# Places for the attention's transposes, scores, probabilities and values, and a later norm product in RWKV

## The chip, the cores and the metric

One core of one Trainium2 chip runs the whole kernel in one launch. The metric is the device time of an execution in microseconds. A profiled execution also has a span, from its first instruction to its last, and a trace of every engine: PE (TensorE matmuls) with its weight loads (PEld), DVE (VectorE), ACT (ScalarE), POOL (GpSimd) and SP (SyncE, which here only issues DMAs).

## The reference

A decoder block over 512 tokens of width 2048, in float32, of depth 1. RWKV-7 time mixing and sliding-window attention run side by side on one projection, their outputs are gated and merged, and a gated ConvFFN follows.

```python
h = rms_norm(x, norm1_g)
z = h @ w_in                               # 2048 columns in; r, k, v, loras, q, k, v, gates out
o_rw = rwkv7_mix(token_shift(z[...]), ...) # 16 heads of 64; a state of 64x64 per head, step by step
o_att = swa_attention(q, k, v, ...)        # 16 query heads on 4 key heads, window 128, sinks
x = x + (sigmoid(zr) * (o_rw @ w_branch[:1024]) + sigmoid(za) * (o_att @ w_branch[1024:])) @ w_out
x = x + conv_ffn(rms_norm(x, norm2_g), w_up, conv_w, conv_b, w_down)

# in rwkv7_mix: kk is normalised per head before the recurrence
kk = kk / max(sqrt(sum(kk * kk)), 1e-12)
# in swa_attention: q and k are normalised per head (rms_norm), then
scores = q @ k.T / 8 + alibi;  p = softmax([scores, sink]);  o = p @ v
```

## The kernel before

Every weight matrix is read from DRAM as float32 and split into a high part (`whi`, ACT) and a rest (`wlo`, DVE). Each product is then three matmuls: high by high, high by rest, rest by high. For the first projection `project` does this per output tile of 128 columns: four weight groups (`load_w`, one DMA `raw` of 256 KB on SP, one ACT step, one DVE step, four buffers each) with 12 matmuls of 128x512 each. These matmuls, in the order in which they are written, are the list `stream`. There are 48 for an output tile. They fill PE while everything else of the branch stage (attention and RWKV) waits on other engines.

The branch work is placed between them. Tile's planner sets the order on each engine from the program and its own costs; `behind(ins, before)` adds that `ins` does not stand ahead of `before` in the order, with no semaphore, and `pin` keeps the written order among the pinned instructions. The list `held` collects pairs of an instruction and a place in `stream`; at the end each is put behind that matmul. So a number in `at`, `LEVEL` or `CHUNK` says behind how many stream matmuls a step may first stand, counted from the pair's `base`; `lag` moves a pair's places later. Engines take their queues in order: what stands first and waits holds what is behind it.

Attention, stream matmuls 0 to 720: for each of ten key and query tiles `qk_norm` squares the tile, `head_stats` sums the squares per head on PE, `rsqrt_small` takes the root on DVE in some twelve tiny steps, and `head_rows` transposes the 8 roots on PE, copies them (`rsT`), writes them to DRAM (`rsd`) and reads them back spread over the partitions (`rsb`, two DMAs on SP behind the first). Then for each of 4 groups and 4 blocks: scores (`scp`), a softmax on DVE and ACT (`sc`, `pr`), transposes of the probabilities (`mi`) and values by probabilities (`mi` from `phi` and `plo`). Three PSUM buffers `mi` go round between roots, probabilities and values.

RWKV works on eight pairs of heads. `early(p)` makes a pair's operands, `late(p)` does the recurrence in 8 chunks of 64 tokens. `early(p + 1)` is written behind `late(p)`, and both run beside each other. In `late`, a chunk n is a chain over three engines: `psG` (PE), `GY` (ACT), `psU` (PE), `UV` (half on ACT, half on DVE), `psS` (PE), and the state's update `SV` (DVE), on which the next chunk's `psG` depends. In `early`, `kk` is multiplied by the roots `rsb` on DVE (the line `kk, kk, rb`), and `kz`, `BKK` and `BAR` are made from it. `bon` and the tile `lw` are other DVE steps there; `BAR` and `BKK` are the operands of the next pair's grams (`bulk`).

Behind the last pair, pass B multiplies the branches' outputs by `w_branch` (with `project` again), and the output product `o`, then the ConvFFN, follow. For `o`, `steps_of` loads factors (`hraw`) and splits them (`hhi` on ACT, `hlo` on DVE). The first two are loaded and split while pass B still runs.

Of the kernel before, what the change touches and what calls it, by code (L numbers as in the profile page):

```python
# [14 lines left out]
ALU = mybir.AluOpType  # L15
# [4 lines left out]
P = 128  # L20
# [115 lines left out]
def block_kernel(ctx: ExitStack, tc: tile.TileContext, d: Dims, a: dict, out: bass.AP):  # L136
# [76 lines left out]
        return ins  # L213

    def split(hi, lo, src, pin=free):
        pin(act.activation(hi, src, AF.Copy))
        pin(dve.tensor_tensor(lo, src, hi.bitcast(F32) if hi.dtype == F32R else hi, op=ALU.subtract))


    def quarter(w, src, c):  # L220
# [31 lines left out]
    def behind(ins, before):  # L252
        tc.add_manual_dep(ins.ins, before.ins.name,
                          mybir.DependencyInfo(mybir.DependencyClass.NoSync, mybir.DependencyReason.DATA))

    def load_w(src):
        nk, ncol = src.shape[1:]
        n = nk * ncol
        raw = wp["raw"].tile([P, 512], F32, name="raw", tag="raw")[:, :n].rearrange("p (k c) -> p k c", c=ncol)
        wp["last"] = sync.dma_start(raw, src)  # L260
        hi = wp["hl"].tile([P, 512], F32R, name="whi", tag="whi")[:, :n].rearrange("p (k c) -> p k c", c=ncol)
        lo = wp["hl"].tile([P, 512], BF16, name="wlo", tag="wlo")[:, :n].rearrange("p (k c) -> p k c", c=ncol)
        act.activation(hi, raw, AF.Copy)  # L263
        dve.tensor_tensor(lo, raw, hi.bitcast(F32), op=ALU.subtract)  # L264
# [31 lines left out]
    if True:  # L296
# [96 lines left out]
        def head_stats(ps, sq):  # L393
            dst = ps[:, 0 : 2 * NT].rearrange("p (h t) -> p t h", h=2)
            for t in range(NT):
                pe.matmul(dst[:, t], sq[:, t * P : (t + 1) * P], K["sel2"], start=True, stop=True)

        def head_rows(pl, ps, rs, tag="lg", bufs=1):
            pe.transpose(ps[0 : 2 * NT, 0:P], rs, ident)
# [3 lines left out]
            sync.dma_start(rd, sm)  # L403
            rb = pl.tile([P, S], F32, name="rsb", tag=tag, bufs=bufs)
            src = rd.rearrange("(h t) c -> h (t c)", h=2)
            for h in range(2):
                sync.dma_start(rb[h * HD : (h + 1) * HD], src[h : h + 1].to_broadcast([HD, S]))
            return rb


        with ExitStack() as pt:
# [4 lines left out]
            def small():  # L416
                return mps.tile([P, S], F32, name="mi", tag="mi")

            unscaled = []

            def finish():

                if unscaled:
                    dst, z, rb, then = unscaled.pop()
                    pin(dve.tensor_tensor(dst, z, rb, op=ALU.mult))
                    then()

            def qk_norm(acc, gain, dst, then=lambda: None, raw=False):
                z = ap_.tile([P, S], F32, name="zq", tag="zq", bufs=3)
                if raw:  # L430
                    dve.tensor_tensor(z, acc, rowb, op=ALU.mult)
                else:
                    dve.tensor_scalar(z, acc, gain, None, op0=ALU.mult)
                sq = ap_.tile([P, S], F32, name="sqq", tag="sqq", bufs=2)
                act.activation(sq, z if raw else acc, AF.Square)
                if raw:
                    dve.tensor_scalar(z, z, gain, None, op0=ALU.mult)
                ps = small()
                head_stats(ps, sq)
                rs = rsqrt_small(ap_, ps[:, 0 : 2 * NT], 1.0 / HD, RMS_EPS)  # L440
                rb = head_rows(ap_, small(), rs, bufs=2)
                finish()
                unscaled.append((dst, z, rb, then))

# [55 lines left out]
            for g in range(NHK):  # L500
# [7 lines left out]
                for n in range(NT):  # L508
# [4 lines left out]
                    for j in range(GQ // 2):  # L513
                        for e in range(2):
                            hs = slice(e * HD, (e + 1) * HD)
                            pe.matmul(scp[e][:, j, k0:], qn[j][hs, ts],
                                      kd[g][hs, n * P - BLK + k0 : (n + 1) * P], start=True, stop=True)
# [23 lines left out]
                    for kb in kbs:  # L541
                        ps = small().rearrange("p (h c) -> p h c", c=P)
                        for h in range(GQ):
                            pe.transpose(ps[:, h % 2 * (GQ // 2) + h // 2], pr_[:, h, kb * BLK : (kb + 1) * BLK], ident)
                        split(phl[0][:, kb], phl[1][:, kb], ps)
                    ps = small()
                    for kb in kbs:
                        for i in range(2):
                            pe.matmul(ps, vhl[:, n - 1 + kb, g].rearrange("p e c -> p (e c)"),  # L549
                                      phl[i][:, kb].rearrange("p h c -> p (h c)"),  # L550
                                      start=kb == kbs[0] and i == 0, stop=kb == kbs[-1] and i == 1)
# [8 lines left out]
        with ExitStack() as pr:  # L560
# [21 lines left out]
            def bulk():  # L582
                return blk.tile([P, S], F32, name="bulk", tag="bulk")
# [41 lines left out]
            def r3(ap, c=C):  # L625
                return ap.rearrange("p (n c) -> p n c", c=c)

            def early(p):
# [12 lines left out]
                sq = wtile("lg")  # L641
                act.activation(sq, kk, AF.Square)
# [40 lines left out]
                pin(dve.tensor_tensor(kk, kk, rb, op=ALU.mult))  # L683
                dve.tensor_tensor(kb, kk, ta, op=ALU.mult)
# [4 lines left out]
                dve.tensor_tensor(bon, vz, ps, op=ALU.mult)  # L689
                return ag, Ei, kk, kb, k2, rz, vz, bon  # L690

            def late(p, st, norm, finish):
                ag, Ei, kk, kb, k2, rz, vz, bon = st
# [151 lines left out]
                for n in range(NCH):  # L845
# [21 lines left out]
                            entries.append(ins)  # L867
                    if n < NCH - 1:
                        for h, (lo, hi) in enumerate(HV):
                            dve.scalar_tensor_tensor(SV[lo:hi, n + 1, h], SV[lo:hi, n, h], ee[lo:hi, n : n + 1],  # L870
                                                     s2[lo:hi, n % HN, h], op0=ALU.mult, op1=ALU.add)
# [41 lines left out]
                dve.tensor_tensor(yc, yc, ps, op=ALU.mult)  # L913
                pool.dma_start(o_rw_d[p], yc)

            entries, grams = [], []
# [28 lines left out]
        with tc.tile_pool(name="ain", bufs=1, side="right", reuse_waits="tile") as ainp:  # L945
# [137 lines left out]
    def steps_of(w, i, acc, c, pl, got=None, flat=None):  # L1083
# [538 lines left out]
```

## Time and profile before

| what | value |
|---|---|
| median of 3 runs | 2703.35 us (2701.12 to 2705.6) |
| profiled execution, time | 2707.28 us |
| its span | 2705.4 us |
| granted TensorE clock, mean | 0.997 |
| PE busy | 2663.3 us, 98% |
| DVE, ACT, POOL busy | 2053.8, 1329.4, 458.0 us |
| attention beside the stream | about 50 to 245 us of the span |
| RWKV pairs | about 280 to 1060 us |
| pass B, output product | from about 1100 us |
| ConvFFN | from about 1450 us |

How to read it: busy PE time is matmul time, whose ends are modelled, so PE at 98% is not PE at its peak, but a hole in it is a hole. The stages have different limits; a wait counts only where PE has nothing else to do. A wait for several semaphores is put down to the one that came last.

### The profile page before, as it was taken

Reading aid. Unit: us, or ns where it says so; the run is one execution under the profiler, and the core shown is the slowest. Engines: PE = TensorE matmul, PEld = TensorE weight load, DVE = VectorE, ACT = ScalarE, POOL = GpSimd, SP = SyncE. Lnnn points to the kernel's source line nnn. Section 1 sums busy time; section 2 is a strip of 40 time slices with the busy share of each in tenths; the row PEclk is TensorE's granted clock in tenths of the full one; section 3 lists DMA queues with packets and bytes.
Section 4 is the critical chain, followed back from the end, with each engine's and each line's share of the span. In section 5 each row is a group of like instructions: output and inputs, shape, how many; then the busy total and the mean of one; then the engine's idle time right before and its main releaser. Section 6 shows DMA issues by size and latency. Waiting matters only on the chain.

```text
span 2705.4 us, 46047 instructions
## 1 busy us (share of the span) xinstructions
PE 2663.3 (98%) x17426; PEld 1870.3 (69%) x17426; DVE 2053.8 (76%) x3387; ACT 1329.4 (49%) x2229; POOL 458.0 (17%) x455
## 2 busy tenths in 40 slices
PE   8999999999999999999999999999999999999999
PEld 5555566666666666555558999999999998555555
DVE  8787758767777874545678888888888888688887
ACT  6455435445544543322456555555555555444443
POOL 0001111011111001111000111111111110166665
PEclk9999999999999999999999999999999999999999
DMA  5566888788888777878785988988898888877885
GB/s 174 157 160 186 226 202 211 192 227 218 212 211 225 193 181 180 288 240 291 255 283 164 253 243 249 255 239 237 245 253 239 237 248 258 316 248 247 265 263 190
DMA packets 227759, 619.63 MB, mean 229 GB/s; under 512 B 24896, under 2 KB 45008, under 8 KB 227024
## 3 DMA queue, kind: packets, MB, share of 16 engines
q1 hardware_dynamic: 158976, 441.03, 49.6%
q0 software_dynamic: 37216, 136.33, 26.2%
q10 hardware_dynamic: 31344, 39.31, 4.2%
q8 instruction: 137, 2.24, 0.3%
q14 instruction: 86, 0.70, 0.1%
HBM read 566.96 MB, written 191.18 MB: 280 GB/s over the span
## 4 chain that ended last, share of the span: by engine, by line
PE 90%; DVE 5%; DMA 3%; issue 1%; ACT 1%; SPq 0%; DVEq 0%; ACTq 0%; POOL 0%; POOLq 0%
PE acc L284 29%; PE X L1244 18%; PE X L1107 11%; PE Y L1107 9%; PE Y L1244 9%; PE Z L1244 4%; PE psS L864 1%; PE psG L848 1%; DMA rsb<-rsd 1%; PE bulk L770 1%; PE bulk L719 1%; DVE wlo L264 1%; PE mi L549 1%; DMA raw<-in_w_z_dram 1%; PE bulk L786 1%
## 5 line engine op out<-in xcount | busy, mean ns | idle before, releaser
L1094 DVE TENSOR_TENSOR wlo<-raw,whi 128x1024 bf16<-128x1024 f32 x210 | 308.4, 1473 | 93.2 <-ACT whi L1093 92.5
L284 PE MATMUL acc<-xhi,whi 128*128 128x512 f32 x1152 | 348.8, 427 | 9.2 <-ACT whi L263 8.9
L263 ACT ACTIVATE whi<-raw 128x512 fp32r<-128x512 f32 x352 | 218.7, 627 | 278.0 <-PE acc L284 144.8
L1093 ACT ACTIVATE whi<-raw 128x1024 fp32r<-128x1024 f32 x210 | 214.9, 1053 | 274.5 <-POOL w L1098 158.5
L264 DVE TENSOR_TENSOR wlo<-raw,whi 128x512 bf16<-128x512 f32 x352 | 239.8, 688 | 139.1 <-ACT whi L263 118.0
L284 PE MATMUL acc<-xlo,whi 128*128 128x512 bf16 x1152 | 317.3, 382 | 0.0
L284 PE MATMUL acc<-xlo,wlo 128*128 128x512 bf16 x1072 | 292.3, 380 | 0.4 <-DVE wlo L264 0.4
L1244 PEld LDWEIGHTS <-wlo 128*128 128x128 bf16 x2464 | 237.6, 96 | 39.6 <-DVE wlo L1226 0.7
L1098 POOL COPY w<-whi 128x1024 bf16<-128x1024 bf16 x132 | 224.7, 1727 | 177.1 <-ACT whi L1093 177.1
L284 PEld LDWEIGHTS acc<-xhi,whi 128*128 128x128 f32 x1152 | 213.6, 191 | 58.5 <-ACT whi L263 9.4
L1244 PEld LDWEIGHTS <-whi 128*128 128x128 bf16 x2464 | 228.0, 98 | 33.1 <-issue 0.2
L284 PEld LDWEIGHTS <-wlo 128*128 128x128 bf16 x1408 | 137.6, 99 | 151.9 <-issue 9.0
L284 PEld LDWEIGHTS <-whi 128*128 128x128 bf16 x1408 | 126.5, 101 | 149.6 <-issue 48.1
L1226 DVE TENSOR_TENSOR wlo<-raw,whi 128x1024 bf16<-128x1024 f32 x184 | 224.2, 1220 | 6.2 <-ACT whi L1224 6.1
L1224 ACT ACTIVATE whi<-a 128x1024 fp32r<-128x1024 f32 x124 | 130.7, 1054 | 191.6 <-DVE a L1219 188.3
L1224 ACT ACTIVATE whi<-raw 128x1024 fp32r<-128x1024 f32 x184 | 193.1, 1051 | 41.7 <-issue 22.2
L1226 DVE TENSOR_TENSOR wlo<-a,whi 128x1024 bf16<-128x1024 f32 x124 | 151.9, 1225 | 72.0 <-ACT whi L1224 72.0
L243 POOL DMA_DIRECT2D s_dn<-in_w_dn_dram x88 | 72.7, 827 | 773.3 <-DMA s_dn<-s_dn 350.3
L1244 PE MATMUL X<-b,whi 128*128 128x256 f32 (+1 forms) x1472 | 195.2, 280 | 0.2 <-DVE x L1122 0.2
L1244 PE MATMUL Y<-t,whi 128*128 128x256 f32 (+1 forms) x1408 | 186.2, 280 | 0.0
L1244 PE MATMUL X<-t,whi 128*128 128x256 bf16 (+1 forms) x1408 | 185.4, 280 | 0.0
L1297 DVE SCALAR_TENSOR_TENSOR c<-u,par,c 128x512 f32<-128x512 f32 x176 | 131.7, 749 | 40.7 <-ACT c L1288 40.7
(396 smaller groups left out, 4718.4 us busy)
## 6 DMA issues: line engine op xcount, KB each, us to landing
raw<-in_w_up_dram SPq DMA_DIRECT2D x170, 512.0 KB, 5.3
raw<-in_w_z_dram SPq DMA_DIRECT2D x288, 256.0 KB, 5.1
s_dn<-in_w_dn_dram POOLq DMA_DIRECT2D x88, 512.0 KB, 7.0
raw<-s_dn SPq DMA_DIRECT2D x88, 512.0 KB, 4.3
raw<-in_w_up_dram POOLq DMA_DIRECT2D x80, 512.0 KB, 8.4
raw<-in_w_dn_dram SPq DMA_DIRECT2D x66, 512.0 KB, 4.4
s_dn<-in_w_dn_dram SPq DMA_DIRECT2D x44, 512.0 KB, 7.2
s_dn<-s_dn SPq DMA_DIRECT2D x44, 512.0 KB, 10.5
```

The source lines that it names most:

```text
L243: return lambda: pool.dma_start(dst, second, accum_op=ALU.add, max_dma_last_dim=4096)
L263: act.activation(hi, raw, AF.Copy)
L264: dve.tensor_tensor(lo, raw, hi.bitcast(F32), op=ALU.subtract)
L284: stream.append(pe.matmul(acc, l, r, start=k0 + j == 0, stop=k0 + n == nk and j == len(ops) - 1))
L1093: act.activation(whi, wr, AF.Copy)
L1094: dve.tensor_tensor(wlo, wr, whi.bitcast(F32), op=ALU.subtract)
L1098: pool.tensor_copy(w16, top(whi))
L1107: pe.matmul(dst, l, r, start=fst and j == order[0], stop=lst and j == order[2], skip_group_check=True)
L1224: pin(act.activation(hi, t, AF.Copy))
L1226: return lambda: pin(dve.tensor_tensor(lo, t, hi.bitcast(F32), op=ALU.subtract))
L1244: pin(pe.matmul(ps, l, r, start=start and k == 0 and i == way[0], stop=k == KH - 1 and i == way[2], skip_group_check=True))
L1297: pin(dve.scalar_tensor_tensor(t, u[:, i, j + 1 : j + 1 + S], cw[:, j + 1, ci : ci + 1], t, op0=ALU.mult, op1=ALU.add))
```

## The change

Four edits, all of the order alone.

1. Attention: the roots' transposes of the ten norms, the first score matmul of five blocks, the first probability transpose of two, and the first value matmul of all sixteen get places in `stream`.
2. RWKV: in `early`, the product of `kk` and `rsb` is put behind the state's update of chunk 3 of the pair that runs (`states[3]`), and the roots' transpose of the next pair gets a place, `base + lag + 182`. Pair 0 gets places for its sums and its transpose, and its grams move from 11 to 15. The lags of pairs 0 to 3 go from 8, 4, 0, 0 to 10, 7, 4, 2.
3. The branch outputs' splits ahead of pass B alternate with the last gate tiles by threes in place of twos.
4. The first two factor splits of the output product are put behind the last weight split of pass B.

```diff
         hi = wp["hl"].tile([P, 512], F32R, name="whi", tag="whi")...
-        act.activation(hi, raw, AF.Copy)
+        wp["whi"] = act.activation(hi, raw, AF.Copy)
...
         def head_rows(pl, ps, rs, tag="lg", bufs=1):
-            pe.transpose(ps[0 : 2 * NT, 0:P], rs, ident)
+            wp["turn"] = pe.transpose(ps[0 : 2 * NT, 0:P], rs, ident)
...
+            turned_at = [174, 228, 275, 317, 358, 402, 481, 499, 575, 594]
+            values_at = [406, 410, 448, 460, 501, 507, 544, 556, 598, 602, 632, 644, 654, 673, 691, 708]
+            scores_at = {(0, 1): 389, (0, 2): 396, (1, 2): 494, (2, 1): 581, (2, 2): 588}
+            probs_at = {(1, 2): 541, (3, 2): 690}
+            placed = []
...
                 rb = head_rows(ap_, small(), rs, bufs=2)
+                placed.append((wp["turn"], turned_at.pop(0)))
...
-                head_stats(ps, sq)
+                stats = head_stats(ps, sq)
                 rs = rsqrt_small(wk, ps[:, 0 : 2 * NT], None, None, mx=1e-24)
                 rb = head_rows(wk, bulk(), rs, "lg")
+                turn = wp["turn"]
+                if p == 0:
+                    placed.extend([(stats, 885), (turn, 896)])
...
-                pin(dve.tensor_tensor(kk, kk, rb, op=ALU.mult))
+                ins = pin(dve.tensor_tensor(kk, kk, rb, op=ALU.mult))
+                if state:
+                    behind(ins, state)
...
-                            dve.scalar_tensor_tensor(SV[lo:hi, n + 1, h], ...)
+                            ins = dve.scalar_tensor_tensor(SV[lo:hi, n + 1, h], ...)
+                        states.append(ins)
...
+            LAG = [10, 7, 4, 2] + [0] * NP
...
-                    st = early(p + 1)
+                    st = early(p + 1, states[3])
...
-                lag = max(0, 8 - 4 * p)
+                lag = LAG[p]
...
-                    held.append((grams[0], base + 11))
+                    held.append((grams[0], base + 15))
+                if p + 1 < NP:
+                    held.append((st[-1], base + lag + 182))
...
                 split(rhi[:, i], rlo[:, i], rin[i], pin)
-                if i % 2:
+                if i % 3 == 2 or i == NP - 1:
                     emit_gate()
             while gates:
                 emit_gate()
+            held += [(ins, n - 1) for ins, n in placed]
...
         if not got:
-            make()
+            ins = make()
+            if w == "o" and i == 0 and c < 2:
+                behind(ins, wp["whi"])
```

What the planner makes of it. First DVE in pair 0's recurrence, where the operands of pair 1 are made (`kk<-kk,rsb` is the product by the roots, `UV` and `SV` are the running chunks). Before:

```order
L870 SCALAR_TENSOR_TENSOR SV<-SV,ee,psS 64x64 x2
L217 TENSOR_TENSOR rk_4083<-lw,rk_4082 128x512
L683 TENSOR_TENSOR kk<-kk,rsb 128x512
L689 TENSOR_TENSOR bon<-vz,bulk 128x512
L684 TENSOR_TENSOR kz<-kk,at__3916 128x512
L264 TENSOR_TENSOR wlo<-raw,whi 128x512
L856 COPY UV<-psU 64x64
```

Here the `UV` is that of chunk 2. After:

```order
L878 COPY UV<-psU 64x64
L265 TENSOR_TENSOR wlo<-raw,whi 128x512
L892 SCALAR_TENSOR_TENSOR SV<-SV,ee,psS 64x64 x2
L899 TENSOR_TENSOR yc<-GY,psS 64x256 x2
L702 TENSOR_TENSOR kk<-kk,rsb 128x512
L705 TENSOR_TENSOR kz<-kk,at__3916 128x512
L721 TENSOR_TENSOR BKK<-kz,Ei 64x8x64
L878 COPY UV<-psU 64x64
```

The product now stands behind the update of chunk 3 and the first half's output `yc`, and the `UV` behind it is that of chunk 4; in pairs 3 and 4 a `wlo` and `kz` stand between, in pair 2 `kz` alone, in the last three pairs a `wlo` alone.

Next PE at the same pair, at the roots' transpose (`bulk<-ident,rq`). Before, between `psU` and `psS` of chunk 0:

```order
L853 MATMUL psU<-GY,BX 128x128
L284 LDWEIGHTS wlo
L284 MATMUL acc<-xlo,wlo 128x512
L284 LDWEIGHTS whi
L284 MATMUL acc<-xlo,whi 128x512
L399 MATMUL bulk<-ident,rq_3874 8x128
L650 MATMUL bulk<-wl,thw 128x128 x4
```

After, between `psG` and `psU` of chunk 1:

```order
L285 MATMUL acc<-xhi,whi 128x512 x2
L870 MATMUL psG<-SV,BAR 128x64 x2
L285 MATMUL acc<-xhi,whi 128x512 x3
L403 MATMUL bulk<-ident,rq_3874 8x128
L669 MATMUL bulk<-wl,thw 128x128 x4
L285 MATMUL acc<-xhi,whi 128x512 x2
L875 MATMUL psU<-GY,BX 128x128
```

The transpose has moved from behind stream matmul 1141 to behind 1153, and the lora product next to it has moved along; in the later pairs it is 12 to 16 places too.

Last ACT near the end of pass B (`whi` from `raw` of 512 is pass B's weight, of 1024 the output product's). Before, in the middle of the pass:

```order
L263 ACTIVATE whi<-raw 128x512 x6
L216 ACTIVATE hhi<-hraw 128x512
L263 ACTIVATE whi<-raw 128x512
L1032 DMA gin<-gate_d 128x512 x3
L263 ACTIVATE whi<-raw 128x512
```

After, the first `hhi` is here:

```order
L264 ACTIVATE whi<-raw 128x512
L1122 ACTIVATE whi<-raw 128x1024
L264 ACTIVATE whi<-raw 128x512
L216 ACTIVATE hhi<-hraw 128x512 x2
L1122 ACTIVATE whi<-raw 128x1024
```

Both early factor splits now stand behind pass B's last weight split.

More of the change, by code (lines that the diff above doesn't have):

```diff
@@ L215, in split @@
     def split(hi, lo, src, pin=free):
-        pin(act.activation(hi, src, AF.Copy))
+        ins = pin(act.activation(hi, src, AF.Copy))
         pin(dve.tensor_tensor(lo, src, hi.bitcast(F32) if hi.dtype == F32R else hi, op=ALU.subtract))
+        return ins
     def quarter(w, src, c):
@@ L395, in head_stats @@
             for t in range(NT):
-                pe.matmul(dst[:, t], sq[:, t * P : (t + 1) * P], K["sel2"], start=True, stop=True)
+                ins = pe.matmul(dst[:, t], sq[:, t * P : (t + 1) * P], K["sel2"], start=True, stop=True)
+                if t == 0:
+                    first = ins
+            return first
         def head_rows(pl, ps, rs, tag="lg", bufs=1):
-            pe.transpose(ps[0 : 2 * NT, 0:P], rs, ident)
+            wp["turn"] = pe.transpose(ps[0 : 2 * NT, 0:P], rs, ident)
             sm = pl.tile([2 * NT, P], F32, name="rsT", tag="rsT", bufs=2)
@@ L515, in block_kernel @@
                             hs = slice(e * HD, (e + 1) * HD)
-                            pe.matmul(scp[e][:, j, k0:], qn[j][hs, ts],
-                                      kd[g][hs, n * P - BLK + k0 : (n + 1) * P], start=True, stop=True)
+                            ins = pe.matmul(scp[e][:, j, k0:], qn[j][hs, ts],
+                                            kd[g][hs, n * P - BLK + k0 : (n + 1) * P], start=True, stop=True)
+                            if j + e == 0 and (g, n) in scores_at:
+                                placed.append((ins, scores_at[g, n]))
                     sc = ap_.tile([P, GQ, 2 * BLK], F32, name="sc", tag="sc", bufs=2)
@@ L543, in block_kernel @@
                         for h in range(GQ):
-                            pe.transpose(ps[:, h % 2 * (GQ // 2) + h // 2], pr_[:, h, kb * BLK : (kb + 1) * BLK], ident)
+                            ins = pe.transpose(ps[:, h % 2 * (GQ // 2) + h // 2], pr_[:, h, kb * BLK : (kb + 1) * BLK], ident)
+                            if h == 0 and kb == kbs[0] and (g, n) in probs_at:
+                                placed.append((ins, probs_at[g, n]))
                         split(phl[0][:, kb], phl[1][:, kb], ps)
@@ L548, in block_kernel @@
                         for i in range(2):
-                            pe.matmul(ps, vhl[:, n - 1 + kb, g].rearrange("p e c -> p (e c)"),
-                                      phl[i][:, kb].rearrange("p h c -> p (h c)"),
-                                      start=kb == kbs[0] and i == 0, stop=kb == kbs[-1] and i == 1)
+                            ins = pe.matmul(ps, vhl[:, n - 1 + kb, g].rearrange("p e c -> p (e c)"),
+                                            phl[i][:, kb].rearrange("p h c -> p (h c)"),
+                                            start=kb == kbs[0] and i == 0, stop=kb == kbs[-1] and i == 1)
+                            if kb == kbs[0] and i == 0:
+                                placed.append((ins, values_at.pop(0)))
                     ol = ap_.tile([HD, S], F32, name="ol", tag="ol", bufs=2)
@@ L626, in r3, with early @@
                 return ap.rearrange("p (n c) -> p n c", c=c)
-            def early(p):
+            def early(p, state=None):
                 wl = lp.tile([P, 2 + NG, P], F32, name="wl", tag="wl", bufs=1)
@@ L689, in early @@
                 dve.tensor_tensor(bon, vz, ps, op=ALU.mult)
-                return ag, Ei, kk, kb, k2, rz, vz, bon
+                return ag, Ei, kk, kb, k2, rz, vz, bon, turn
             def late(p, st, norm, finish):
-                ag, Ei, kk, kb, k2, rz, vz, bon = st
+                ag, Ei, kk, kb, k2, rz, vz, bon, _ = st
+                states.clear()
                 Eex, Ein = Et[:, :, 0:C], Et[:, :, 1:]
@@ L869, in late @@
                         for h, (lo, hi) in enumerate(HV):
[L870 to L871 removed]
+                            ins = dve.scalar_tensor_tensor(SV[lo:hi, n + 1, h], SV[lo:hi, n, h], ee[lo:hi, n : n + 1],
+                                                           s2[lo:hi, n % HN, h], op0=ALU.mult, op1=ALU.add)
+                        states.append(ins)
                     if n % HN == HN - 1:
@@ L914, in final @@
                 pool.dma_start(o_rw_d[p], yc)
-            entries, grams = [], []
+            entries, grams, states = [], [], []
             LEVEL = [36, 51, 64, 77, 89, 102, 116, 131, 144, 159]
             CHUNK = [171 + 14 * n + 4 * (n > 2) + x for n in range(NCH) for x in (-5, 0, 4)][1:]
+            LAG = [10, 7, 4, 2] + [0] * NP
             st, lt, held = early(0), None, []
```

## The prediction

> **What bounds the kernel now.** I read the page's busy shares first, then the stages in slices of 50 us (columns: slice, length, then busy us and instruction count of PE, PEld, DVE, ACT and POOL, granted clock, DMA share, GB/s), then what PE itself waited for.
>
> ```profile
> PE 2663.3 (98%) x17426; PEld 1870.3 (69%) x17426; DVE 2053.8 (76%) x3387; ACT 1329.4 (49%) x2229; POOL 458.0 (17%) x455
> ...
> 350.00:400.00 50.00, 43.88 (x263) 30.20 (x260) 28.04 (x70) 16.96 (x39) 4.67 (x7) 0.93 0.83 204
> 450.00:500.00 50.00, 45.25 (x266) 30.96 (x266) 28.99 (x72) 18.80 (x43) 6.18 (x9) 0.93 0.88 216
> 650.00:700.00 50.00, 46.85 (x272) 32.71 (x271) 31.95 (x80) 16.53 (x40) 6.91 (x11) 1.00 0.86 224
> 850.00:900.00 50.00, 49.91 (x281) 33.58 (x281) 38.82 (x85) 20.41 (x50) 5.32 (x9) 1.00 0.72 176
> 2000.00:2050.00 50.00, 50.00 (x440) 45.60 (x439) 41.69 (x51) 27.04 (x38) 6.04 (x7) 1.00 0.91 244
> ```
>
> PE is the bound: 2705.4 - 2663.3 leaves 42 us in which it does nothing, and from about 900 us on nearly none of that. So a microsecond of PE waiting that goes in the first 900 us comes off the end. The largest holes are in the RWKV pairs, and two of those slices also have less than the full clock. PE's waits by cause (us in total, times, longest):
>
> ```profile
> PE psS L864 <- DVE UV L856: 14.0, 5, 5.7
> PE acc L284 <- ACT whi L263: 9.9, 3, 7.8
> PE bulk L399 <- DVE rq L207: 3.3, 8, 0.5
> PE mi L399 <- DVE rq L207: 1.6, 4, 0.5
> PE bulk L396 <- ACT lg L642: 1.0, 1, 1.0
> ...
> PE bulk L719 <- DVE bon L689: 0.6, 1, 0.6
> PE mi L399 <- DVE st L530: 0.4, 2, 0.2
> ```
>
> One of the five psS waits in the timeline (start, duration, engine, line, what; in brackets the idle time before and its end), with the chain behind it:
>
> ```profile
> 362.78 0.27 PE L399 MATMUL bulk<-ident,rq 128*8 128x128 f32 x1 [0.40 <-DVE rq L207]
> 364.15 1.00 SPq L403 DMA_DIRECT2D rsd<-rsT  x1
> 372.02 1.11 SPq L407 DMA_DIRECT2D rsb<-rsd  x2
> 378.45 0.69 DVE L683 TENSOR_TENSOR kk<-kk,rsb 128x512 f32<-128x512 f32 x1 [5.82 <-DMA rsb<-rsd]
> 379.18 0.69 DVE L689 TENSOR_TENSOR bon<-vz,bulk 128x512 f32<-128x512 f32 x1
> 379.78 0.68 DVE L684 TENSOR_TENSOR kz<-kk,at__3916 128x512 f32<-128x512 f32 x1
> 380.38 0.69 DVE L264 TENSOR_TENSOR wlo<-raw,whi 128x512 bf16<-128x512 f32 x1
> 381.10 0.23 DVE L856 COPY UV<-psU 64x64 f32<-64x64 f32 x1
> 381.38 1.11 PE L864 MATMUL psS<-UV,W 128*128 128x64 f32 x4 [5.73 <-DVE UV L856]
> ...
> DVE kk L683 <- DMA rsb<-rsd: 15.7, 5, 5.8
> ```
>
> The transpose of the norm's roots goes through DRAM and back (rsd, then rsb). DVE stands 5.8 us at kk until rsb lands, and the running pair's UV copy is fourth in the queue behind it; chunk 2's psS waits for that. DVE's five waits at kk (15.7 us) and PE's five at psS (14.0 us) are the same events.
>
> **The change part by part.** No instruction is added or taken out; only places move.
>
> *A. kk goes behind the fourth SV update.* UV of chunks 2 and 3 no longer stand behind it. The 14.0 us of psS waits go, if rsb has landed when DVE reaches kk. Is it there? I take the undisturbed sixth pair for the pace:
>
> ```profile
> 843.63 0.39 PE L853 MATMUL psU<-GY,BX 128*128 128x128 f32 x2
> 844.44 0.27 PE L399 MATMUL bulk<-ident,rq 128*8 128x128 f32 x1 [0.42 <-DVE rq L207]
> 845.02 0.23 DVE L856 COPY UV<-psU 64x64 f32<-64x64 f32 x1
> 846.40 0.55 PE L864 MATMUL psS<-UV,W 128*128 128x64 f32 x4
> 863.67 0.59 DVE L870 SCALAR_TENSOR_TENSOR SV<-SV,ee,psS 64x64 f32<-64x64 f32 x2 [0.75 <-PE psS L864]
> 864.18 0.85 DVE L876 TENSOR_TENSOR yc<-GY,psS 64x256 f32<-64x256 f32 x2
> 866.41 0.23 DVE L856 COPY UV<-psU 64x64 f32<-64x64 f32 x1 [0.37 <-ACT UV L855]
> 866.82 0.55 PE L864 MATMUL psS<-UV,W 128*128 128x64 f32 x4
> ```
>
> DVE would come to kk after yc, at 864.18 + 0.85 = 865.0. The transpose is now 12 stream matmuls later, behind psS and psG; at 0.22 to 0.25 us a piece and 0.4 us for each of the two it stands at about 847.8, if psS starts at 845.3, when UV is copied. So DVE needs kk some 17 us after the transpose. The slowest chain seen, above, landed 378.45 - 362.78 = 15.7 us after it. That leaves 1.5 us, so I take all 14.0; the bound below is in the rivals.
>
> *B. The clock.* Behind the 5.7 us hole the clock is halved:
>
> ```profile
> 380.00:382.00 2.00, 0.62 (x3) 0.62 (x4) 1.94 (x5) 0.00 (x0) 0.81 (x1) 0.54 0.00 0
> 382.00:384.00 2.00, 2.00 (x7) 1.71 (x7) 1.89 (x5) 0.03 (x1) 0.00 (x0) 0.50 0.78 110
> 384.00:386.00 2.00, 2.00 (x8) 1.61 (x8) 1.34 (x3) 0.60 (x1) 0.00 (x0) 0.50 0.98 196
> 386.00:388.00 2.00, 2.00 (x10) 1.13 (x10) 0.65 (x2) 0.59 (x2) 0.61 (x2) 0.75 1.05 286
> ```
>
> PE works 0.62 + 2 + 2 + 1 = 5.6 us at half speed, 2.8 us lost. The slice from 450 us has the same 0.93, so I take the same again: 5.6 us in all, gone with the holes. The slice from 650 us has its hole (3.1 us idle in all) and the full clock. [...]
>
> *C. The roots' transposes of the pairs, 12 places later.* 3.3 us of waits at them. But the next psS comes nearer: psU at 843.63, four stream matmuls (0.9 us), psS due near 844.8, UV copied only at 845.25; the 0.4 us then stands there. Where UV is now ahead of the last steps of the root (pairs 1 to 4) it goes. Behind the transpose, the product on lw has four or five stream matmuls less to hide its ACT and DVE steps. Between 3.3 us and a loss of 1, I take 1.0. The places of levels and chunks in pairs 0 to 3 move 2 to 4 stream matmuls later and end at the same one; that costs nothing while PE has weights, and takes small waits away that I leave out.
>
> *D. Pair 0:* squares' sums 6 stream matmuls later (1.3 us against 1.0 waited), grams 4 later (0.9 against 0.6). Of 1.6 us I take 1.5.
>
> *E. The first split of the output product goes behind pass B's last weight split.*
>
> ```profile
> 1204.32 0.63 ACT L216 ACTIVATE hhi<-hraw 128x512 fp32r<-128x512 f32 x1 [9.88 <-DMA hraw<-h_o]
> ...
> 1205.52 1.19 PE L284 MATMUL acc<-ahi,whi 128*128 128x512 f32 x4 [0.98 <-ACT whi L263]
> ```
>
> ACT stood 9.9 us for a load with the next weight split behind it; PE ran dry. 1.0 us goes; the split is due only after pass B, with four weight groups of work ahead of PE. The rest of that acc wait (7.8 us) is the kernel's start and stays. Two pairs of branch splits that become triples are hidden by the same four groups: nothing.
>
> *F. Attention.* 1.6 + 0.4 us at transposes. The transposes move by 2 to 9 stream matmuls, more than the waits; but probabilities and values move by up to 18, three PSUM buffers go round between them, and they may be awaited in turn. At most 2.0 us; on the other side six new waits like the longest (0.5), 3 us. I take 1.5, nearer to the gain since each move is later and PE has other work in the gap.
>
> *G. New waits.* After kk come one or two more DVE steps of 0.69 us before chunk 4's UV. One puts UV at 865.03 + 0.69 + 0.69 = 866.4, just as now; two (pairs 1, 3 and 4) make psS, due at 866.82, about 0.5 us late. With 0.5 for a late rsb: 2.0 us lost, between 0 and the first rival's price.
>
> Sum: 14.0 + 5.6 + 1.0 + 1.5 + 1.0 + 1.5 - 2.0 = 22.6 us. The profiled execution, 2707.28 with its span of 2705.4, would come to 2684.7; it lies 3.9 above the median of the runs. From 2703.35 I get 2680.8, say 2681.
>
> **The rivals.** *First: the wait comes back one chunk later.* If rsb lands later than 17 us after the transpose, DVE stands at kk again and chunk 4's UV with it.
>
> ```profile
> SPq L407 <- DMA rsd<-rsT: 54.4, 17, 7.0
> ...
> raw<-in_w_z_dram SPq DMA_DIRECT2D x288, 256.0 KB, 5.1
> ```
>
> The wait for rsd is 3.2 us in the mean and up to 7.0, so it hangs on what else is moving. A weight load of 256 KB now stands just ahead of rsd in the later pairs' queue, and between rsd and rsb in pair 1. If it adds its 5.1 us to the slowest chain, kk stands 15.7 + 5.1 - 17 = 3.8 us in up to four pairs: 15 back, 2696; with half of that, 2688. For it: the loaded slices from 450 and 650 us (0.86 to 0.88 DMA). Against: before, such a load went out less than 1 us ahead of rsd too. [...]
>
> *Second, slower:* the same place, at a higher price. Once kk stands over 4 us the clock is halved as well, and a pair costs some 4.3 + 2.8 = 7 us. It decides at a landing 21 us after the transpose, in four pairs: 28 us, more than the whole gain: 2709. No chain in the rows is that long.
>
> *Third: attention gives it back.* DVE is nearly full there; 3 us lost in place of 1.5 won, and a start of RWKV that follows attention's later end (its last store now stands one accumulating DMA later on POOL, ahead of the memsets of RWKV): 2686.
>
> *Fourth: the change does not do what it says.* A place is only a lower bound, and if DVE meets another late operand ahead of UV, the psS waits stay and only small terms are left: 2700. Against it: in the new DVE order nothing ahead of UV 2 and 3 comes from a DMA but wlo.
>
> **How the numbers follow.** Forecast 0.62 (2674 to 2685); first 0.16; third 0.11; fourth 0.06; second 0.05. About 0.2%, 5.4 us, is what a measurement of this kernel tells from no change. Faster: 0.62 + 0.16 + 0.11 = 0.89; same 0.06; slower 0.05. The low end has terms C to F whole and G at nothing, 27.5 us and the 1.4 of the clock: 2674. The high end, 2693, takes in most of the first rival and all of the third.
>
> **What would show it.** psS waits for UV near 2 us in total, and PE's rows at chunk 4 (not 2) if any; DVE at kk waiting for rsb under 2 us in sum; clock 1.00 in the slices from 350 and 450 us; no acc wait near 1200 us; L399 under 1 us. It is wrong if kk still waits over 2 us in several pairs, if a slice there is under 1.00, or if PE's idle time between 50 and 250 us grows.

## The result and the profile after

The changed kernel takes 2690.79 us in the median of six runs (2685.59 to 2696.97), the kernel before, beside it, 2704.88 us (2701.12 to 2708.59). The ratio is 0.9945, with a 95% interval of 0.9928 to 0.9963. It is faster, as forecast, by 14.1 us where 22.6 were forecast. The profiled execution (2696.97 us, span 2695.2) is the slowest of the six, so its holes may well be larger than those of a usual execution. One later execution of the changed kernel, in d3 below, ran at a granted clock of 0.851 and took 2953 us; it is left out of the ratio there, and why it ran so is not known.

The page's busy shares and the slices of 50 us, in the columns used before:

```profile
PE 2662.9 (99%) x17426; PEld 1867.2 (69%) x17426; DVE 2057.3 (76%) x3387; ACT 1332.8 (49%) x2229; POOL 459.2 (17%) x455
```

```profile
150.00:200.00 50.00, 46.07 (x219) 26.75 (x218) 38.74 (x119) 21.81 (x66) 3.27 (x4) 0.93 0.58 153
200.00:250.00 50.00, 47.13 (x217) 26.34 (x216) 43.08 (x108) 30.09 (x89) 2.41 (x3) 0.97 0.37 101
350.00:400.00 50.00, 49.84 (x346) 32.96 (x345) 34.81 (x86) 22.72 (x48) 6.33 (x9) 1.00 0.91 233
450.00:500.00 50.00, 49.78 (x310) 33.12 (x306) 34.05 (x83) 20.75 (x49) 8.26 (x13) 1.00 0.91 228
```

The RWKV slices are full now, at the full clock: 49.84 and 49.78 us busy where 43.88 and 45.25 were. Two attention slices have got worse. Before, they read:

```profile
150.00:200.00 50.00, 48.60 (x251) 28.59 (x251) 45.45 (x142) 26.29 (x80) 3.27 (x4) 1.00 0.56 146
200.00:250.00 50.00, 49.43 (x237) 27.97 (x237) 42.57 (x103) 30.71 (x87) 5.74 (x9) 1.00 0.54 145
```

PE idles (3.93 + 2.87) - (1.40 + 0.57) = 4.8 us more there, and the granted clock is 0.93 and 0.97 in place of 1.00. PE's longest waits by cause in the changed kernel, and one of DVE's:

```profile
PE acc L285 <- ACT whi L264: 9.0, 2, 7.9
PE mi L556 <- DVE st L542: 5.7, 2, 3.2
PE bulk L741 <- DVE W L748: 3.2, 1, 3.2
PE psS L886 <- DVE UV L878: 1.7, 4, 0.6
```

```profile
DVE qn L434 <- DMA rsb<-rsd: 6.8, 3, 3.1
```

The psS waits have gone from 14.0 to 1.7 us and there is no DVE wait at kk at all. In their place stand two waits of PE at the probabilities' transposes (L556), one at pair 0's grams (L741), and three of DVE at the attention's `qn`, the query tile multiplied by its roots. The timeline of the place in pair 0 that the prediction walked through:

```profile
375.97 0.27 PE L403 MATMUL bulk<-ident,rq 128*8 128x128 f32 x1
...
392.26 0.68 DVE L702 TENSOR_TENSOR kk<-kk,rsb 128x512 f32<-128x512 f32 x1
...
394.41 0.23 DVE L878 COPY UV<-psU 64x64 f32<-64x64 f32 x1
...
394.83 0.55 PE L886 MATMUL psS<-UV,W 128*128 128x64 f32 x4
```

DVE comes to kk 16.3 us after the transpose; the roots are there, and psS of chunk 4 follows its UV with no idle time in its brackets. Now the same place in attention, at the seventh norm (norm 6, counting from 0) beside group 1's first block:

```profile
146.09 0.27 PE L403 MATMUL mi<-ident,rq 128*8 128x128 f32 x1
...
147.25 0.51 SPq L407 DMA_DIRECT2D rsd<-rsT  x1
147.80 1.00 SPq L243 DMA_DIRECT2D s_o<-in_w_o_dram  x1
153.99 1.12 SPq L411 DMA_DIRECT2D rsb<-rsd  x2
...
153.68 1.20 DVE L539 TENSOR_REDUCE st<-sc 128x4 f32<-128x1024 f32 x1
157.96 0.69 DVE L434 TENSOR_TENSOR qn<-zq,rsb 128x512 f32<-128x512 f32 x1 [3.08 <-DMA rsb<-rsd]
159.51 0.69 DVE L549 TENSOR_TENSOR pr<-pr,st 128x512 f32<-128x512 f32 x1
...
160.35 0.63 PE L556 MATMUL mi<-ident,pr 128*128 128x128 f32 x4 [3.24 <-DVE st L542]
```

This is the picture that the change removed from RWKV. DVE stands at a product whose roots are still on their way through DRAM, and what PE needs, here the probabilities' product `pr`, is behind it. DVE gets there at 153.68 + 1.20 = 154.88, 8.8 us after the transpose; the roots land 11.9 us after it. Before, the order was the other one:

```profile
146.60 0.27 PE L399 MATMUL mi<-ident,rq 128*8 128x128 f32 x1 [0.43 <-DVE rq L207]
...
155.40 0.68 DVE L537 TENSOR_TENSOR pr<-pr,st 128x512 f32<-128x512 f32 x1
...
156.74 0.67 DVE L425 TENSOR_TENSOR qn<-zq,rsb 128x512 f32<-128x512 f32 x1
```

`pr` stood ahead of `qn`, which DVE reached 10.1 us after the transpose, without a wait. The other hole (2.44 us) is the same at norm 8. Pair 0's hole is of the same kind with another load (ACT, DVE and PE in the timeline):

```profile
321.39 0.63 ACT L264 ACTIVATE whi<-raw 128x512 fp32r<-128x512 f32 x1 [6.37 <-DMA raw<-in_w_z_dram]
...
322.06 0.69 DVE L265 TENSOR_TENSOR wlo<-raw,whi 128x512 bf16<-128x512 f32 x1 [3.13 <-ACT whi L264]
...
323.00 0.42 DVE L748 TENSOR_TENSOR W<-bulk,cst 128x256 f32<-128x256 f32 x1
...
323.56 1.10 PE L741 MATMUL bulk<-BAR,BKK 128*128 128x256 f32 x4 [3.19 <-DVE W L748]
```

A weight split whose load is late stands on DVE ahead of `W`, the step that frees the grams' buffer.

### The profile page after: what moved, and what is told of

Its sections match the earlier page's. It is cut to its first block, busy times and chain, and to the rows that moved or that the text cites. A ratio compares the mean times of both kernels' runs of the same rounds, so it can differ in the third digit from the quotient of the medians.

```text
span 2695.2 us, 46025 instructions
## 1 busy us (share of the span) xinstructions
PE 2662.9 (99%) x17426; PEld 1867.2 (69%) x17426; DVE 2057.3 (76%) x3387; ACT 1332.8 (49%) x2229; POOL 459.2 (17%) x455
## 4 chain that ended last, share of the span: by engine, by line
PE 90%; DVE 4%; DMA 2%; issue 2%; ACT 2%; SPq 0%; POOL 0%; DVEq 0%; ACTq 0%; POOLq 0%
PE acc L285 29%; PE X L1273 18%; PE X L1136 11%; PE Y L1136 9%; PE Y L1273 9%; PE Z L1273 4%; PE psS L886 1%; PE psG L870 1%; PE bulk L741 1%; PE bulk L792 1%; DVE wlo L265 1%; PE mi L563 1%; PE scp L526 1%; PE bulk L808 1%; PE psU L875 0%
```

## The experiments

My theory: RWKV's part does what was forecast, and attention gives back some 8 us, because the places of the roots' transposes put `qn` ahead of `pr` in DVE's queue and leave its trip through DRAM too little time. The rival: RWKV's gain is itself only some 14 us, and attention costs no more than before. In the next four kernels parts of attention's edit are taken out, or stand alone. Each set of these experiments had a chip of its own, with the kernel before beside it. So medians of one set compare directly; across sets the ratios are the safer measure.

```diff
# a1: no attention place, pair 0's stay
-            held += [(ins, n - 1) for ins, n in placed]
+            held += [(ins, n - 1) for ins, n in placed if n > 720]
# a2: no places for the ten transposes
-                placed.append((wp["turn"], turned_at.pop(0)))
# a3: all places, and behind the probabilities' product of block 0 of groups 1 and 2
+                    if n == 0 and g in (1, 2):
+                        behind(wp["scaled"], ins)   # scaled: the last qn
# a4: the kernel before with the attention places alone (edits 2 to 4 undone)
```

> The changed kernel without any place for attention (edits 2 to 4 stay). Theory: the gain that is missing is lost in attention, where PE stood 3.2 and 2.4 us for probabilities whose product waited on DVE behind a normalised query tile (qn), and where the clock fell to 0.93 and 0.97. Without the places those two holes and the half clock go: about 2680 us, clock 1.00 in the slices from 150 and 200 us, 'PE mi <- DVE st' under 1 us. Rival: the gain of RWKV is itself only some 14 us, and attention loses as much before as after: 2690 us, no change to the changed kernel.

> The changed kernel without the places of the ten norms' root transposes alone; the places of scores, probabilities and values stay. Theory: the transposes' places are what puts qn ahead of the probabilities' product in DVE's queue (without them a probabilities' product and a zq step stand between the copy of the roots and qn, as before the change); 2680 us, no wait of DVE at qn for rsb. Rival: the places of values and probabilities make PE wait in turn through the three mi buffers: about 2690 us, as the changed kernel.

> The changed kernel with one order added: the qn product of norms 6 and 8 goes behind the probabilities' product of block 0 of the group that runs. All places stay. Theory: what PE waits for is the probabilities' product behind qn, not the later transposes themselves: the two holes go although qn may still wait 1 us or so for its roots: 2680 to 2683 us. Rival: the trip of the roots through DRAM, which starts 2.6 to 6.8 us later at norm 8, holds what comes next on DVE or the scores of the next group: 2690 us or above, with the hole at another instruction.

> The kernel before with the attention places alone (edits 2 to 4 undone). Theory: slower by what the profile shows in the slices from 150 and 200 us, 12.6 us of lost time, less 1 us won at the transposes: about 2715 us; less where an execution's holes are too short to halve the clock (2708 to 2711). Rival: attention's places cost nothing by themselves, and the holes came with the rest of the change: 2703 to 2705 us.

| kernel | median us | ratio to before (95%) |
|---|---|---|
| before, beside them | 2703.54 | |
| a1, no attention places | 2685.31 | 0.9935 (0.9921 to 0.9948) |
| a2, no transposes' places | 2682.55 (2681.86 to 2682.82) | 0.9921 (0.9909 to 0.9934) |
| a3, qn behind pr | 2685.91 | 0.9939 (0.9924 to 0.9954) |
| a4, attention places alone | 2708.59 (2701.83 to 2710.59) | 1.0009 (0.9995 to 1.0024) |

a2 settles which list it is. With scores, probabilities and values still placed, the time is 8.2 us under the changed kernel's; its five runs lie within 1 us, all below every run of the changed kernel. a1 against a2 shows that those other places are worth 2.8 us, so my 2680 for a1 was too low. a3 keeps the late transposes and only turns the order on DVE. In its trace the two holes at the probabilities are gone (PE's longest wait there is 0.5 us). Its median lies 4.9 us under the changed kernel's, short of the 2680 to 2683 expected; but the ratios, 0.9939 and 0.9945, cannot be told apart, so how much of the cost goes with the order alone is not shown. The 3.4 us to a2, on the same chip, stay. a4 came out at neither 2715 nor the rival's 2703 to 2705, but in the 2708 to 2711 expected for short holes; by its interval it cannot be told from the kernel before. In its profiled execution attention lost nothing. The order is that of the changed kernel, but the trip was short:

```profile
146.10 0.27 PE L403 MATMUL mi<-ident,rq 128*8 128x128 f32 x1
...
147.25 0.29 SPq L407 DMA_DIRECT2D rsd<-rsT  x1
147.59 0.50 SPq L243 DMA_DIRECT2D s_o<-in_w_o_dram  x1
151.16 1.12 SPq L411 DMA_DIRECT2D rsb<-rsd  x2
...
154.85 0.69 DVE L434 TENSOR_TENSOR qn<-zq,rsb 128x512 f32<-128x512 f32 x1
```

DVE comes at the same 8.75 us after the transpose, and does not wait. Between `rsd` and `rsb` lie 3.9 us here and 6.7 us in the changed kernel's profile, with the same load between them on SP. A second profile of the changed kernel itself (d3, below) has 4.8 us, again with that load between, and `qn` there waits 0.96 us. So the price of this order differs from execution to execution: almost nothing here, holes of 1.4 and 0.5 us at the full clock in d3, holes of 3.2 and 2.4 us with half the clock behind them in the first profile.

The second set takes RWKV apart, and asks which of the ten transposes hurt.

```diff
# b1: the kernel before with only this
+                if state:
+                    behind(ins, state)          # state = states[3]
# b2: a2, with kk a chunk earlier
-                    st = early(p + 1, states[3])
+                    st = early(p + 1, states[2])
# b3: a2, without the next pair's transpose's place and the new lags
-                    held.append((st[-1], base + lag + 182))
...
-            LAG = [10, 7, 4, 2] + [0] * NP
+            LAG = [8, 4, 0, 0] + [0] * NP
# b4: the changed kernel, the last four norms' transposes without a place
-                placed.append((wp["turn"], turned_at.pop(0)))
+                turn = turned_at.pop(0)
+                if turn < 481:
+                    placed.append((wp["turn"], turn))
```

> The kernel before with one edit alone: kk's product behind the state's update of chunk 3. No other place, lag or split is changed. By the prediction's terms A and B the five psS waits (14.0 us) and the half clock (5.6 us) go: 2704 - 19.6 = 2684 us, psS waits under 2 us, clock 1.00 in the slices from 350 and 450 us, and the roots' transposes still wait their 3.3 us. Rival: the places that go with it (transposes 12 matmuls later, lags) are needed too, since kz and BKK come late for the next grams: 2690 us or more.

> The changed kernel without the attention transposes' places (2682.6 us above) with kk's product behind the state's update of chunk 2 in place of chunk 3. Theory: what counts is when DVE reaches kk after the transpose: some 17 us behind chunk 3 (16.3 to 17.3 in the profile of the changed kernel), some 12 to 13 behind chunk 2, and the roots of the slowest pairs land 13 to 16 us after it. So kk waits again, 1 to 4 us in two or three of the pairs, with PE's hole at chunk 3: 2685 to 2690 us. Rival: the roots land within 12 us now that the transposes stand elsewhere, and chunk 3 was not needed: 2682 to 2683 us.

> The changed kernel without the attention transposes' places (2682.6 us above), and the next pair's roots' transposes and the lags as in the kernel before. Theory: the transposes wait for the root again, 8 times 0.4 us = 3.3 us, and psS at UV less: 2683.5 (net 1.0, as predicted) to 2686 us (all of 3.3). Rival: the waits at the transposes were paid back elsewhere in full, and nothing changes: 2682.5 us.

> The changed kernel with the places of the first six norms' transposes and none for the last four. In this order the probabilities' product and the zq step stand ahead of qn again at norms 6 and 8. Theory: only those two norms are short of time; the first six places save two or three waits of 0.47 us: 2681.5 to 2682.5 us, as the kernel without any of the ten or a little less. Rival: the earlier places lengthen the trips of norms 2 and 3 as well (qn 10.5 us after the transpose in place of 11.6), and a hole appears there: 2685 us or more.

| kernel | median us | ratio to before (95%) |
|---|---|---|
| before, beside them | 2706.10 | |
| b1, kk's place alone | 2689.08 | 0.9940 (0.9926 to 0.9955) |
| b2, kk behind chunk 2 | 2696.96 (2690.98 to 2705.64) | 0.9969 (0.9952 to 0.9986) |
| b3, old root places | 2683.01 | 0.9916 (0.9900 to 0.9931) |
| b4, first six transposes' places | 2681.94 | 0.9915 (0.9898 to 0.9931) |

b1: one `behind` gives 17.0 us in the medians, and its profiled span (2686.2) is 19.2 us under that of before. This one edit does as well as the whole changed kernel (0.9940 against 0.9945), though its median is 5 us above the 2684 expected and close to the rival's 2690. No psS wait is left among PE's waits; the transposes still wait their 3.3 us:

```profile
PE bulk L403 <- DVE rq L207: 3.3, 8, 0.5
```

```profile
350.00:400.00 50.00, 49.62 (x307) 33.99 (x306) 34.37 (x85) 19.93 (x46) 6.12 (x10) 1.00 0.90 226
450.00:500.00 50.00, 49.49 (x271) 33.66 (x271) 36.08 (x90) 18.98 (x44) 6.09 (x10) 1.00 0.88 225
```

b2 shows how narrow the choice of chunk 3 was. One chunk earlier costs 14.4 us against a2 (13 by the ratios), and the runs spread over 15 us. Waits, the timeline in pair 2 and the clock in stretches of 2 us, from its profile:

```profile
PE psS L885 <- DVE UV L877: 7.1, 8, 2.1
DVE kk L701 <- DMA rsb<-rsd: 6.7, 5, 2.4
```

```profile
548.38 0.27 PE L403 MATMUL bulk<-ident,rq 128*8 128x128 f32 x1
...
561.79 0.69 DVE L701 TENSOR_TENSOR kk<-kk,rsb 128x512 f32<-128x512 f32 x1 [2.44 <-DMA rsb<-rsd]
```

```profile
564.00:566.00 2.00, 0.68 (x3) 0.68 (x4) 1.94 (x5) 0.00 (x0) 1.38 (x3) 0.81 0.29 27
566.00:568.00 2.00, 2.00 (x8) 0.90 (x8) 1.92 (x6) 0.00 (x0) 0.00 (x0) 0.50 0.89 184
568.00:570.00 2.00, 2.00 (x12) 1.32 (x11) 1.27 (x2) 0.27 (x1) 0.00 (x0) 0.84 0.99 261
```

DVE came to kk 11.0 us after the transpose (561.79 - 2.44 - 548.38), and the roots landed 13.4 us after it. The profiled execution, the quickest of them (2690.98), has 7.1 us of waits and half a clock behind one hole; the longer ones presumably had more of either, which no trace here shows. My 2685 to 2690 was too low for the median. b3 is the same as a2: the later transposes of the pairs are worth nothing that can be measured. b4 is as good as a2; only the last four norms' places hurt. From b1 to b4 lie 7.2 us. The parts seen one by one, the other attention places (2.8), pair 0 and the splits (1.6 and 0.9, below) and the later transposes (nothing), make 5.3; the rest is not located.

The third set sizes two small terms from b4, and runs the changed kernel once more beside them.

```diff
# d1: b4, with pair 0's sums, transpose and grams (base + 11) where they were
# d2: b4, with the branch splits by twos and the early output splits where they were
# d3: the changed kernel itself
```

> The kernel with the first six transposes' places (2681.9 us above), with pair 0's sums, transpose and grams where the kernel before has them (the prediction's term D undone). The prediction gave D 1.5 us: 2683.4. Theory now: up to stream matmul 1141 the kernel with kk's place alone was 4.3 us behind the one with the old root places, 1.3 of it in attention, so D is worth about 3 us: 2685. Rival: D costs, as the hole of 3.2 us in pair 0's grams in the changed kernel's profile would have it: 2680 us.

> The kernel with the first six transposes' places (2681.9 us above), with the branch outputs' splits by twos and the output product's two early splits where the kernel before has them (the prediction's term E undone). The prediction gave E 1.0 us: 2682.9, with a wait of PE at acc for whi near 1180 us of 0.7 to 1 us. Rival: the wait comes back but PE makes it up, since the next weights are ready: 2681.9 us.

> The changed kernel itself, once more, beside the two others on one chip. Theory: its attention waits hang on when the roots of norms 6 and 8 land, so its times spread over some 10 us (2685 to 2697 so far, where the kernel without the late transposes' places spread over 1 us), with a median 6 to 9 us above 2682. Rival: the first six times were a poor draw, and it lies within 3 us of the others.

Before, beside them, took 2704.5 us; d1 2683.51 (0.9918, 0.9905 to 0.9932), d2 2682.84 (0.9917, 0.9904 to 0.9931), d3 2690.30 (0.9942, 0.9928 to 0.9955). d1 and d2 lie 1.6 and 0.9 us above b4 in the medians (0.8 and 0.5 by the ratios, b4 having run on another chip). Terms D and E said 1.5 and 1.0, but the intervals overlap with b4's, so this is agreement and no proof. In d2 the wait near 1180 us that was expected did not appear; PE waited 1.1 us for a branch split (`rlo`) at 1089 instead. Its profile also has a hole of 1.7 us at pair 0's grams, in which the splits have no part. d3 confirms the changed kernel: 8.4 us above b4, and 6.8 and 7.5 us above d1 and d2 beside it. PE's waits in its profile (2687.83 us) are of the same two kinds as in the first, but shorter:

```profile
PE bulk L741 <- DVE W L748: 2.3, 1, 2.3
PE mi L556 <- DVE st L542: 1.9, 2, 1.4
```

So the 8 us that the four transposes' places cost are not attention's alone: some of it stands at pair 0's grams.

Last, the two causes crossed: early transposes, but `pr` forced behind `qn`.

```diff
# e1: a2, and
+                    if n == 0 and g in (1, 2):
+                        behind(ins, wp["scaled"])   # ins: the probabilities' product
```

> The kernel without any of the ten transposes' places (2682.6 us above) with the opposite order forced: the probabilities' product of block 0 goes behind qn of norms 6 and 8, as the changed kernel has it; the transposes stay early. With this the two causes are crossed: late transposes with qn first (the changed kernel, 2690.5), late with qn behind (2685.9), early with qn behind (2682.6), early with qn first (this). Theory: what costs is that DVE comes to qn 8.6 to 8.8 us after the transpose and the roots land later than that; here it comes some 9.5 us after it, since zq still stands ahead, and the roots land 10 us after it, so qn waits up to 1 us twice: 2683 to 2685 us. Rival: the order by itself is the cost, wherever the transposes stand: 2688 us or more.

It took 2687.66 us (0.9940, 0.9927 to 0.9954), 5.1 us above a2 and close to the rival's figure. But the profile puts the loss elsewhere (slices, and one row of PE's waits):

```profile
150.00:200.00 50.00, 48.57 (x244) 28.29 (x244) 44.36 (x141) 26.46 (x79) 4.08 (x5) 1.00 0.65 172
200.00:250.00 50.00, 49.38 (x239) 28.42 (x238) 42.88 (x102) 30.67 (x87) 4.74 (x8) 1.00 0.53 132
```

```profile
PE bulk L742 <- DVE W L749: 2.8, 1, 2.8
```

Attention is whole in that execution: at norm 6 DVE came to `qn` 10.1 us after the transpose and did not wait. Pair 0's grams have the hole. So e1 does not decide between order and lateness. By the ratios a3, e1 and d3 (0.9939, 0.9940, 0.9942) cannot be told apart, and only a2, with neither, is clear of them in its runs. What makes pair 0's weight load late stays open. From its issue on SP to its split it took 9.0, 8.0, 8.4 and 8.8 us where there was a hole (the changed kernel, d3, e1, d2: 3.2, 2.3, 2.8 and 1.7 us) and 4.9 to 5.9 us where there was 0.2 us or none (a1, a2, a3, b4). d2 and b4 have the same order up to there, so it is not the order alone. Whether the last four transposes' places make it likelier is not shown.

## Why the prediction was right, and what it mis-sized

**A and B, kk and the clock: right.** 14.0 + 5.6 = 19.6 us were forecast for the profiled execution; kk's place alone gave 19.2 between profiled spans. In the medians it gave 17.0. That is a step that failed in the arithmetic: I took the profiled execution's holes off the median (2703.35 - 22.6), though that execution lay 3.9 us above it, perhaps because its holes were larger than usual, which is not shown. The low end of the range, 2674, takes off 1.4 us more for the clock, and no run shows that term; the trace of before shows PE at work for 5.6 us at half speed from 380 us and for 6.0 from 478, behind a hole of 4.25 us (0.06 + 2 + 2 + 1.96 in stretches of 2 us, at 0.79, 0.50, 0.50 and 0.51), 5.8 us lost against the 5.6 taken. The reasoning on time held: DVE came to kk 16.3 us after the transpose where 17 were forecast, and in b2 11.0 us were too few.

**C, transposes of the pairs: near enough.** 1.0 forecast, nothing measurable. The bound that was named is what one sees: the 3.3 us at L403 are gone, and the four psS waits left in the changed kernel (1.7 us) are at chunk 0 of the running pairs 3 to 6, counting from 0 (the first at 649.08), where "the 0.4 us then stands there".

**D, pair 0: in size right, as far as the runs can tell** (1.6 us in d1), and overtaken by a hole of 3.2 us in the changed kernel's profile that I had not foreseen. **E: not shown.** 0.9 us in d2 agrees with the 1.0, but the wait that came back was at a branch split, which I had put at nothing, and not at the output product's, and the hole at pair 0's grams is in d2's times too.

**F, attention: the step that failed.** The term was "I take 1.5, nearer to the gain since each move is later and PE has other work in the gap", with 3 us as the worst. Forecast was a gain of 1.5; by a1 the whole edit costs some 5 us (2690.3 to 2690.8 against 2685.31; 2 to 3 by the ratios), and by b4 the last four transposes 8.4. I looked at PE and at the PSUM buffers only. In A I asked whether the roots are there when DVE comes; here, with the same trip at ten norms, I did not, and I did not look at DVE's order, where `pr` had moved behind `qn`. Nor did I apply B's price to it: in the first profile, the slowest execution, 4.8 us of added idle time have 5.1 us of lost clock behind them (below). In d3's the clock stayed whole.

**G, new waits: too pessimistic.** The 2.0 us at chunk 4 and for a late rsb did not come; no psS wait of the changed kernel is at chunk 4.

**The rivals.** The third, that attention gives the gain back, came true at more than its price: 2686 was forecast, 2690.8 came. Its reason, a full DVE and a later start of RWKV, is not what the traces show; they show `pr` queued behind a product that waits 3.1 and 2.6 us for DRAM. No rival named that, nor pair 0's late load. So the median lies outside the 2674 to 2685 that had the chance of 0.62, and inside the stated range only because its end of 2693 had been stretched for the first and third rivals: for the number, that is luck, while the mechanism of A and B was right. The first did not happen in RWKV, where kk waited for nothing, and its 2696 did not come; in attention a load stands between rsd and rsb in three traces with 3.9, 4.8 and 6.7 us, so the load's place alone does not set the trip. What the prediction named as a sign of its failure, PE idle time growing between 50 and 250 us, is what the profile shows.

In medians: 17.0 (A, B), 7.2 more up to b4 (24.2 under before, beside it), less 8.4 for the four transposes: 15.8 against 14.1 measured on another chip. b4 is the fastest kernel here, at 2681.94 us, with a2 beside it.

## What to carry to other kernels

When a producer is moved later, follow its result to the consumer, on every engine's queue: the question is not whether the moved step waits less, but whether its consumer now comes before the data, and who is queued behind. A wait that hangs on a trip through DRAM has no fixed size: the same order took 3.9, 4.8 and 6.7 us between the two issues in three profiles, so a place that leaves no room is paid for in some executions and not in others. The spread of the runs is a weak sign of it: 15 us in b2 and 1 us in a2, but 3 us in d3, whose trace has such waits, and 5 us in b4. A hole in PE can cost half the clock on top of its length: here one of 2.14 us had 3.4 us of it behind it, and one of 3.19 us none. And take holes off the execution in which they were seen.

## What was not expected of the hardware

The prediction set half the clock behind a hole of 5.7 us beside the full clock of a slice with 3.1 us of idle time (its hole was 2.64 us), and a4's expectation spoke of holes "too short to halve the clock". That the length of a hole decides is not borne out by the changed kernel's stretches of 2 us (PE busy first, the clock third from the end):

```profile
160.00:162.00 2.00, 1.65 (x9) 1.38 (x10) 1.97 (x5) 2.00 (x9) 0.00 (x0) 0.81 0.91 175
162.00:164.00 2.00, 2.00 (x5) 0.79 (x3) 1.41 (x7) 0.55 (x2) 0.00 (x0) 0.50 0.26 87
...
168.00:170.00 2.00, 2.00 (x14) 1.29 (x13) 1.70 (x6) 0.81 (x5) 0.00 (x0) 0.98 0.00 0
204.00:206.00 2.00, 2.00 (x12) 1.12 (x10) 2.00 (x5) 1.50 (x5) 0.46 (x1) 0.91 0.66 129
206.00:208.00 2.00, 2.00 (x6) 0.80 (x6) 2.00 (x9) 0.00 (x0) 0.00 (x0) 0.50 0.98 208
208.00:210.00 2.00, 2.00 (x9) 0.81 (x8) 1.14 (x2) 1.64 (x5) 0.00 (x0) 0.74 0.66 187
320.00:322.00 2.00, 0.37 (x2) 0.00 (x0) 0.00 (x0) 0.61 (x1) 0.00 (x0) 1.00 1.03 389
322.00:324.00 2.00, 0.44 (x2) 0.45 (x3) 1.95 (x6) 0.24 (x2) 0.00 (x0) 1.00 0.60 235
324.00:326.00 2.00, 2.00 (x11) 1.36 (x10) 2.00 (x7) 1.54 (x5) 0.81 (x1) 1.00 0.36 115
```

A stretch at clock c holds 2 x (1 - c) / 0.5 us at half speed: 0.76 + 2 + 2 + 2 + 0.08 = 6.8 us behind the hole of 3.24 us (the two stretches left out read 0.50 as well), 0.36 + 2 + 1.04 = 3.4 us behind that of 2.44, and nothing behind that of 3.19, at 320 to 324. Half of 6.8 + 3.4 is the 5.1 us lost. In b2, 3.4 us followed a hole of 2.14 us (0.76 + 2 + 0.64), in e1 3.4 us one of 2.84 us at pair 0's grams (1.04 + 2 + 0.36), while d3's hole of 2.3 us there and the 2.64 us of the kernel before had none behind them. So between 2 and 3.3 us the length of a hole does not say whether the half clock comes: it came behind 2.14, 2.44, 2.84 and 3.24 us and not behind 2.3, 2.64 and 3.19. The two longer ones in RWKV before, 4.25 and 5.73 us, had 6.8 us of it each. What decides it is not shown.
